# Two x loads ahead of two weight loads, and the pooling's constants in large buffers: a one-layer encoder block on one Trainium2 core

## The chip, the core and the metric

The kernel runs on one core of a Trainium2 chip. A core has five engines that run side by side, each with its own in-order queue of instructions: TensorE (PE in the profile; its weight loads are listed apart as PEld), VectorE (DVE), ScalarE (ACT), GpSimd (POOL) and SyncE (SP). Here SP issues nearly all transfers from device memory, and sixteen DMA engines carry them out. Matmul results go into PSUM banks; everything else lies in the core's on-chip memory, called SBUF.

The metric is the device time of one execution in microseconds (us); lower is better. The time before is 1462.05 us, the median of three runs (1461.95 to 1462.69).

## The reference, cut to what matters

One layer, 256 positions of 2048 channels in float32. The input is normalised, multiplied by one wide matrix into seven parts, mixed by a pooling branch and a retention branch, gated, projected, added, and followed by a gated feed-forward part:

```python
u = rmsnorm(h, norm_mix)
z = u @ w_in                                  # 2048 x 11264
p, q, k, v, g_ret, g_pool_br, g_ret_br = jnp.split(z, split_idx, axis=-1)
y_pool = pool_branch(p, w_pool_group, pool_scale) @ w_pool_proj
y_ret = retention_branch(q, k, v, g_ret, ret_gn_gain) @ w_ret_proj
merged = sigmoid(g_pool_br) * y_pool + sigmoid(g_ret_br) * y_ret
h = h + merged @ w_out
h = h + conv_glu(rmsnorm(h, norm_ffn), w_up, conv_w, conv_b, w_down)
out = rmsnorm(h, norm_final)
```

`rmsnorm` divides each position by the root of its mean square. `pool_branch` takes trailing means over 2, 4, 8 and 16 positions for four groups of channels, subtracts the token itself, and multiplies each group by its own 256x256 matrix.

## The kernel before

**Arithmetic.** Each float32 product is made of three matmuls. `split` (L95) makes a rounded copy `hi` on ACT (L96) and the remainder `lo` on DVE (L97); `mm3` (L103) does hi x hi, lo x hi and hi x lo (L104, L105, L106). In some places a Strassen scheme (`Pair.strassen`, L317) does seven block products instead of eight.

**The z stage.** The columns of `w_in` are taken in eleven pairs of 512-column blocks. Each pair runs over eight groups of 256 rows of weights; one group is one load of 1 MB (128 partitions x 2048 floats). `run_pair` (L370) does a pair: per group and per half (one 512-column block) it multiplies the two 128-row blocks of positions, `tb` 0 and 1, 12 matmuls of 128x512 for each half of a group. In a pair's last two groups the order is turned round: both groups for half 0, then both for half 1, 24 matmuls each. So the two PSUM banks of half 0 are complete 24 matmuls before the pair ends. There are four such banks (`acc`), all in use by one pair, and the next pair's first matmul needs one that has been emptied.

**The first pair** gives the first columns of q and k. It starts with the kernel and its eight groups of weights are loaded, with the transposed x, at the top (L192 to L222; `raws`). Its banks are emptied by four copies on ACT (L498) in `qk_pair`; the rotation of q and k (`rotate`, L510) comes later, since it needs the reciprocal root of the mean square of x.

**That mean square** comes from a second load of x, in the layout with positions on partitions. `x_squares(tb)` (L243) loads one half of x (1 MB, L245) into a large buffer and runs four squares with a sum on ACT (L248); for the second half it also issues the loads of three constant tables (`trig`, `ident`, `vecs`). `x_rms` (L254) adds up the sums, makes the reciprocal root on DVE in 16 small instructions, and scales the rotation's table with it (L260).

**When this is done in the program** is set by the queue `side`: `run_pair` calls `tick` (L139) after each group, and each tick runs the next entry of `side`. An empty entry lets one group pass:

```python
side.extend([lambda: None] * 4)
side.append(lambda: x_squares(0))
side.extend([lambda: None] * 2)
side.append(lambda: x_squares(1))
side.extend([lambda: None] * 2)
side.append(x_rms)
```

**From the program's order to the engines' order.** A scheduler takes the instructions by priority, which follows the program's order; weight loads and their splits are marked with a higher one (`weights_first`, L84; used by `halves_of`, L283), and so are results (`results_first`, L91). What comes out is a fixed order for each engine, and semaphores for what has to wait.

**Buffers.** Weights land in three buffers `raw` (pool `wraw`, L55), and are split into four `hi` and four `lo` buffers of half a group each (pool `wsplit`, L56). A load is issued when the buffer's last content has been split, and a split runs when PE has read the last content of its `hi` and `lo`. Everything large that lives longer lies in 18 buffers of 8 KB per partition (`unit()`, L68). Names in the trace are those of the program: `u` for a large buffer, `t` for a small one (512 floats), `acc` and `aux` for PSUM.

**The pooling** (L666 to L727) starts behind the pair that makes its input. It loads a small table (`cnt`), the pooling's matrix (768 KB, `pm_raw`) and the group weights (1 MB, `wg_raw`); both use `raw` buffers (L668, L672). The matrix is copied once on ACT (L671), the weights are split in two halves (L677). `pool(g)` (L681) and `mix(g)` (L706) then run from `side` in the next pair.

Of the kernel before, what the change touches and what calls it, by code (L numbers as in the profile page):

```python
# [8 lines left out]
F32 = mybir.dt.float32  # L9
# [7 lines left out]
P = 128  # L17
# [31 lines left out]
def tile_block(ctx: ExitStack, tc: tile.TileContext, ins, out):  # L49
# [5 lines left out]
    wraw = ctx.enter_context(tc.tile_pool(name="wraw", bufs=3))  # L55
# [8 lines left out]
    def nm(base):  # L64
        counter[0] += 1
        return f"{base}_{counter[0]}"

    def unit(dt=F32):  # L68
        return units.tile([P, UNIT], dt, tag="u", name=nm("u"))
# [67 lines left out]
    side = deque()  # L137
# [105 lines left out]
    def x_squares(tb):  # L243
        xs = unit()
        sp.dma_start(xs, ins["x"][tb])  # L245
        for c in range(4):
            junk = t2k()
            act.activation(junk, xs[:, c * NB : (c + 1) * NB], AF.Square, accum_out=ssq1[:, tb, c : c + 1])  # L248
        if tb:
            sp.dma_start(trig, ins["trig"])  # L250
            sp.dma_start(ident, ins["ident"])
            sp.dma_start(vecs, ins["vecs"])
# [385 lines left out]
        side.append(lambda: turn((2, 3)))  # L638


    side.extend([lambda: None] * 4)
    side.append(lambda: x_squares(0))
    side.extend([lambda: None] * 2)
    side.append(lambda: x_squares(1))
    side.extend([lambda: None] * 2)
    side.append(x_rms)
    for half in range(2):
        qk = [unit(F32R), unit(F32R)]
# [16 lines left out]
    flush()  # L665
    cnt = const.tile([P, 4, 16], F32, tag="cnt", name="cnt")  # L666
    sp.dma_start(cnt, ins["invcnt"])
    pm_raw = wraw.tile([P, 2048], F32, tag="raw", name="pm_raw")  # L668
    sp.dma_start(pm_raw[:, : 4 * 384], ins["poolmat"])
    pm = unit(F32R)  # L670
    act.activation(pm[:, : 4 * 384], pm_raw[:, : 4 * 384], AF.Copy)  # L671
    wg_raw = wraw.tile([P, 2048], F32, tag="raw", name="wg_raw")  # L672
    sp.dma_start(wg_raw, ins["w_pool_group"])
    wg_h, wg_l = unit(F32R), unit(F32R)
    for i in range(2):
# [491 lines left out]
```

## Time and profile before

| | |
|---|---|
| median of three runs | 1462.05 us |
| the profiled execution, its own time | 1462.85 us |
| span of the core in that execution | 1461.0 us |
| mean granted TensorE clock over the span | 0.996 |
| DMA: moved, mean rate | 291.22 MB, 199 GB/s |

The profile is of one execution. Its span is the time from the core's first to its last event, and the own time has 1.85 us around it. Times within the trace are counted from the span's start. The page gives each engine's busy time; a busy TensorE need not be at full speed, since matmuls overlap (a 128x512 matmul is listed at 0.39 us, while the next one starts 0.23 us behind it) and since the granted clock can fall. So waits and slow stretches are read in two ways: from the idle time that the trace puts ahead of an instruction, with the one that ended it, and from the distance between one matmul's start and the next. In the rows of SP the time is that at which a transfer is issued; when it landed is told apart.

### The profile page before, as it was taken

The numbers are of one execution on the slowest core, as the hardware profiler recorded it, in microseconds if no ns is written. First come the engines' busy times: TensorE is split into PE (matmuls) and PEld (weight loads), VectorE is DVE, ScalarE is ACT, GpSimd is POOL, SyncE is SP. The second block draws the span as 40 slices with busy tenths as digits, with TensorE's granted clock in tenths as the row PEclk, the third lists the DMA queues.
The fourth block names the chain that finished last, engine by engine and source line by source line (L and its number), as shares of the span: only waits on it lengthen the run. The fifth ranks groups of instructions, "written<-read, shape, count | busy, mean of one in ns | idle before, by whom it ended". The sixth has DMA issues, their size and how long they took to land.

```text
span 1461.0 us, 18727 instructions
## 1 busy us (share of the span) xinstructions
PE 1446.0 (99%) x7163; PEld 1222.9 (84%) x7163; DVE 1179.1 (81%) x1638; ACT 794.6 (54%) x1023; POOL 0.2 (0%) x4
## 2 busy tenths in 40 slices
PE   9899999999999999999999999999999999999997
PEld 7788888888888888888888888888888888888886
DVE  6768797987888888988877777777777778888877
ACT  6555654555655554545564554555455445555553
POOL 0000000000000000000000000000000000000000
PEclk9999999999999999999999999999999999999999
DMA  8664456455456556565565554554555456655663
GB/s 317 218 216 173 144 202 223 173 169 227 148 199 222 210 177 219 185 227 214 194 227 183 206 188 173 201 201 174 183 207 187 173 202 237 223 204 187 228 210 122
DMA packets 43289, 291.22 MB, mean 199 GB/s; under 512 B 4928, under 2 KB 5568, under 8 KB 9152
## 3 DMA queue, kind: packets, MB, share of 16 engines
q1 hardware_dynamic: 42480, 288.73, 55.1%
q10 hardware_dynamic: 720, 1.31, 0.3%
q8 instruction: 56, 0.92, 0.2%
q14 instruction: 33, 0.27, 0.1%
HBM read 285.82 MB, written 4.19 MB: 198 GB/s over the span
## 4 chain that ended last, share of the span: by engine, by line
PE 96%; DMA 1%; DVE 1%; ACT 1%; issue 0%; SPq 0%; DVEq 0%; ACTq 0%
PE acc L879 22%; PE acc L104 15%; PE acc L106 15%; PE acc L105 15%; PE acc L887 11%; PE aux L104 6%; PE aux L105 6%; PE aux L106 6%; DMA raw<-in_w_in 1%; DVE lo L97 1%; ACT hi L96 0%; PE aux L526 0%; PE aux L745 0%; PE aux L805 0%; PE aux L623 0%
## 5 line engine op out<-in xcount | busy, mean ns | idle before, releaser
L96 ACT ACTIVATE hi<-raw 128x1024 fp32r<-128x1024 f32 (+1 forms) x522 | 545.7, 1052 | 410.8 <-PE acc L105 184.0
L97 DVE TENSOR_TENSOR lo<-raw,hi 128x1024 fp32r<-128x1024 f32 (+1 forms) x522 | 617.4, 1212 | 159.6 <-ACT hi L96 101.2
L104 PE MATMUL acc<-hi,u 128*128 128x512 f32 x926 | 363.6, 393 | 4.6 <-ACT t L498 3.8
L106 PE MATMUL acc<-lo,u 128*128 128x512 f32 x926 | 361.9, 391 | 0.5 <-DVE lo L97 0.5
L105 PE MATMUL acc<-hi,u 128*128 128x512 f32 x926 | 361.6, 390 | 0.0
L879 PE MATMUL acc<-u,hi 128*128 128x512 f32 x1408 | 328.4, 390 | 0.0
L879 PEld LDWEIGHTS acc<-u,hi 128*128 128x128 f32 x1408 | 261.3, 188 | 52.2
L104 PEld LDWEIGHTS acc<-hi,u 128*128 128x128 f32 x926 | 174.6, 189 | 42.3 <-ACT t L498 4.3
L106 PEld LDWEIGHTS acc<-lo,u 128*128 128x128 f32 x926 | 174.5, 188 | 38.7 <-DVE lo L97 2.3
L105 PEld LDWEIGHTS acc<-hi,u 128*128 128x128 f32 x926 | 174.6, 189 | 35.2
L887 PEld LDWEIGHTS acc<-u,lo 128*128 128x128 f32 x1408 | 174.8, 192 | 3.4
L887 PE MATMUL acc<-u,lo 128*128 128x256 f32 x1408 | 176.0, 283 | 0.0
L104 PE MATMUL aux<-hi,u 128*128 128x512 f32 x270 | 105.2, 390 | 0.0
L105 PE MATMUL aux<-hi,u 128*128 128x512 f32 x270 | 105.1, 389 | 0.0
L106 PE MATMUL aux<-lo,u 128*128 128x512 f32 x270 | 105.1, 389 | 0.0
L901 ACT ACTIVATE t<-acc 128x256 f32<-128x256 f32 x88 | 33.8, 384 | 99.9 <-PE acc L887 99.9
L96 ACT ACTIVATE u<-u 128x1024 fp32r<-128x1024 f32 x43 | 45.5, 1057 | 26.7 <-DVE u L304 21.1
L106 PEld LDWEIGHTS aux<-lo,u 128*128 128x128 f32 x270 | 50.7, 188 | 10.6
L104 PEld LDWEIGHTS aux<-hi,u 128*128 128x128 f32 x270 | 50.7, 188 | 10.5 <-ACT hi L96 0.2
L105 PEld LDWEIGHTS aux<-hi,u 128*128 128x128 f32 x270 | 50.7, 188 | 10.3
L96 ACT ACTIVATE four<-raw 128x512 fp32r<-128x512 f32 x43 | 27.1, 631 | 55.3 <-PE acc L105 20.7
L97 DVE TENSOR_TENSOR u<-t,u 128x256 fp32r<-128x256 f32 (+2 forms) x52 | 27.0, 527 | 37.0 <-ACT u L96 37.0
(183 smaller groups left out, 1127.8 us busy)
## 6 DMA issues: line engine op xcount, KB each, us to landing
raw<-in_w_up SPq DMA_DIRECT2D x88, 1024.0 KB, 5.1
raw<-in_w_in SPq DMA_DIRECT2D x85, 1024.0 KB, 4.9
raw<-in_w_down SPq DMA_DIRECT2D x44, 1024.0 KB, 4.9
raw<-in_w_ret_proj SPq DMA_DIRECT2D x16, 1024.0 KB, 4.9
raw<-in_w_out SPq DMA_DIRECT2D x16, 1024.0 KB, 4.9
raw<-in_w_pool_proj SPq DMA_DIRECT2D x8, 1024.0 KB, 4.9
u<-in_x SPq DMA_DIRECT2D x4, 1024.0 KB, 7.1
raw<-in_w_in SPq DMA_DIRECT2D x4, 512.0 KB, 7.9
```

The costliest lines, as they stand in the source:

```text
L96: act.activation(hi, src, AF.Copy)
L97: dve.tensor_tensor(lo, src, plain(hi), ALU.subtract)
L104: pe.matmul(o, ah, bh, start=start, stop=False)
L105: pe.matmul(o, al, bh, start=False, stop=False)
L106: pe.matmul(o, ah, bl, start=False, stop=stop)
L879: pe.matmul(o[half], w2[half][hf][0][:, i * P : (i + 1) * P], hview(kt), start=kt == 0, stop=False)
L887: pe.matmul(o[half][:, :T], wl, hview(kt)[:, :T], start=False, stop=kt == KT - 1)
L901: act.activation(small_part[:, half * T : (half + 1) * T], o[half][:, T:], AF.Copy)
```

## The change

Two edits. The first moves the two calls of `x_squares` in `side`: they ran at the fifth and eighth tick of the first pair, and now run at the third and fourth. The number of empty entries is chosen so that `x_rms` stays at the eleventh. The second takes `pm_raw` and `wg_raw` from the large buffers instead of the `raw` buffers.

```diff
-    side.extend([lambda: None] * 4)
+    side.extend([lambda: None] * 2)
     side.append(lambda: x_squares(0))
-    side.extend([lambda: None] * 2)
     side.append(lambda: x_squares(1))
-    side.extend([lambda: None] * 2)
+    side.extend([lambda: None] * 6)
     side.append(x_rms)
...
-    pm_raw = wraw.tile([P, 2048], F32, tag="raw", name="pm_raw")
+    pm_raw = unit()
     sp.dma_start(pm_raw[:, : 4 * 384], ins["poolmat"])
...
-    wg_raw = wraw.tile([P, 2048], F32, tag="raw", name="wg_raw")
+    wg_raw = unit()
     sp.dma_start(wg_raw, ins["w_pool_group"])
```

The order of TensorE's instructions stays as it was; the orders of SP, ACT and DVE differ at two places each. Numbers in the names below are those of the tiles (before and after the change the x tiles have other numbers; the weights have the same).

SP in the first pair, before: raw_220 is the last group of the first pair, raw_479, raw_535 and raw_583 are the first three of the second.

```order
L165 DMA raw_220<-in_w_in 128x2048
L273 DMA raw_479<-in_w_in 128x2048
L273 DMA raw_535<-in_w_in 128x2048
L245 DMA u_368<-in_x 128x2048
L273 DMA raw_583<-in_w_in 128x2048
L245 DMA u_426<-in_x 128x2048
L250 DMA trig<-in_trig 128x256
L251 DMA ident<-in_ident 128x128
L252 DMA vecs<-in_vecs 128x216
```

The same place of SP now:

```order
L165 DMA raw_220<-in_w_in 128x2048
L245 DMA u_320<-in_x 128x2048
L273 DMA raw_479<-in_w_in 128x2048
L245 DMA u_354<-in_x 128x2048
L250 DMA trig<-in_trig 128x256
L251 DMA ident<-in_ident 128x128
L252 DMA vecs<-in_vecs 128x216
L273 DMA raw_535<-in_w_in 128x2048
L273 DMA raw_583<-in_w_in 128x2048
```

Both halves of x and the three tables have moved ahead of raw_535, and the first half of x ahead of raw_479 as well.

ACT at the end of the first pair, before. t_439, t_441, t_467 and t_469 are the copies of the first pair's four banks: acc_244 and acc_246 hold half 0, acc_245 and acc_247 half 1. The rows with ssq are the squares.

```order
L96 ACTIVATE hi_537<-raw_535 128x1024
L248 ACTIVATE t_376,ssq_238<-u_368 128x512
L96 ACTIVATE hi_541<-raw_535 128x1024
L248 ACTIVATE t_428,ssq_238<-u_426 128x512
L248 ACTIVATE t_430,ssq_238<-u_426 128x512
L248 ACTIVATE t_432,ssq_238<-u_426 128x512
L248 ACTIVATE t_434,ssq_238<-u_426 128x512
L498 ACTIVATE t_439<-acc_244 128x512
L498 ACTIVATE t_441<-acc_246 128x512
L498 ACTIVATE t_467<-acc_245 128x512
L498 ACTIVATE t_469<-acc_247 128x512
```

The same place of ACT now (the squares of the first half of x stand further ahead, two on each side of the split hi_231<-raw_220, and the split of raw_479 comes just before these rows):

```order
L248 ACTIVATE t_356,ssq_238<-u_354 128x512
L248 ACTIVATE t_358,ssq_238<-u_354 128x512
L248 ACTIVATE t_360,ssq_238<-u_354 128x512
L248 ACTIVATE t_362,ssq_238<-u_354 128x512
L498 ACTIVATE t_439<-acc_244 128x512
L498 ACTIVATE t_441<-acc_246 128x512
L498 ACTIVATE t_467<-acc_245 128x512
L96 ACTIVATE hi_537<-raw_535 128x1024
L96 ACTIVATE hi_541<-raw_535 128x1024
L498 ACTIVATE t_469<-acc_247 128x512
```

The two splits of raw_535 stood ahead of the second half's squares and of all four copies; now they stand behind three of the copies and ahead of the fourth. On DVE the reciprocal root of the mean square has moved ahead of the two lo halves of raw_535.

SP at the pooling, before: raw_2773 is the last group of the pair ahead of it, raw_2882, raw_2916, raw_2966 and raw_3033 are the first four of the pair behind it.

```order
L273 DMA raw_2773<-in_w_in 128x2048
L669 DMA pm_raw<-in_poolmat 128x1536
L673 DMA wg_raw<-in_w_pool_group 128x2048
L273 DMA raw_2882<-in_w_in 128x2048
L273 DMA raw_2916<-in_w_in 128x2048
L273 DMA raw_2966<-in_w_in 128x2048
L273 DMA raw_3033<-in_w_in 128x2048
```

The same place now (u_2863 and u_2867 are the pooling's matrix and weights):

```order
L273 DMA raw_2773<-in_w_in 128x2048
L273 DMA raw_2882<-in_w_in 128x2048
L273 DMA raw_2916<-in_w_in 128x2048
L273 DMA raw_2966<-in_w_in 128x2048
L668 DMA u_2863<-in_poolmat 128x1536
L273 DMA raw_3033<-in_w_in 128x2048
L672 DMA u_2867<-in_w_pool_group 128x2048
```

The next pair's first three groups have moved ahead of both loads of the pooling. On ACT the copy of the matrix now stands between the two splits of raw_2916, and the splits of the pooling's weights behind those of raw_2966; before, all three stood ahead of the splits of raw_2916.

## The prediction, made before the change was timed

> **What bounds the kernel now.** I read the page first, then the waits of TensorE, then the order of time around each of them.
>
> ```profile
> span 1461.0 us, 18727 instructions
> PE 1446.0 (99%) x7163; PEld 1222.9 (84%) x7163; DVE 1179.1 (81%) x1638; ACT 794.6 (54%) x1023; POOL 0.2 (0%) x4
> ```
>
> ```profile
> PE acc L104 <- ACT t L498: 3.8, 1, 3.8
> PE acc L104 <- ACT hi L96: 0.8, 2, 0.6
> PE acc L106 <- DVE lo L97: 0.5, 1, 0.5
> ```
>
> PE is the bound: it is busy for 99% of the span, and the built order of its instructions is the same before and after the change. So only two things can move the time: places where PE waits, and places where it runs slowly. The second block is the list of waits (who <- waited for: total, times, longest); it names the waits for ACT and DVE that matter, one of 3.8 us and two or three short ones. DVE (81%), ACT (54%) and the transfers cost nothing except where they make one of these.
>
> The long wait, in PE's order of time (start, duration, instruction, idle time before it):
>
> ```profile
> 49.80 0.39 PE L105 MATMUL acc<-hi,u 128*128 128x512 f32 x1
> 50.02 0.39 PE L106 MATMUL acc<-lo,u 128*128 128x512 f32 x1
> 54.26 0.79 PE L104 MATMUL acc<-hi,u 128*128 128x512 f32 x1 [3.85 <-ACT t L498]
> 54.85 0.63 PE L105 MATMUL acc<-hi,u 128*128 128x512 f32 x1
> ...
> 59.97 0.46 PE L105 MATMUL acc<-hi,u 128*128 128x512 f32 x1
> 60.27 0.40 PE L106 MATMUL acc<-lo,u 128*128 128x512 f32 x1
> ```
>
> A 128x512 matmul starts every 0.227 us when nothing is in the way (49.80 to 50.02). The first pair of column blocks ends at 50.02, the first matmul of the second pair starts at 54.26, and from there to 59.97 they start every 0.43 us. The stage's windows (time, then PE busy, PEld, DVE, ACT, POOL, granted clock, DMA share) say why:
>
> ```profile
> 50.27:54.26 3.99, 0.14 (x1) 0.00 (x1) 1.65 (x4) 3.99 (x11) 0.00 (x0) 0.88 0.56 193
> 54.26:60.27 6.01, 6.01 (x14) 4.71 (x15) 5.49 (x22) 2.31 (x4) 0.00 (x0) 0.51 0.42 165
> ```
>
> In the wait ACT is busy all the time (3.99 of 3.99 us), and after it the granted clock is 0.51: the wait is paid a second time, in half-speed matmuls. What ACT did:
>
> ```profile
> 36.62 1.06 ACT L96 ACTIVATE hi<-raw 128x1024 fp32r<-128x1024 f32 x1 [1.66 <-PE acc L105]
> 39.34 1.06 ACT L96 ACTIVATE hi<-raw 128x1024 fp32r<-128x1024 f32 x1 [1.66 <-PE acc L105]
> 42.06 1.06 ACT L96 ACTIVATE hi<-raw 128x1024 fp32r<-128x1024 f32 x1 [1.66 <-PE acc L105]
> 44.78 1.06 ACT L96 ACTIVATE hi<-raw 128x1024 fp32r<-128x1024 f32 x1 [1.66 <-PE acc L105]
> 45.75 0.61 ACT L248 ACTIVATE t<-u 128x512 f32<-128x512 f32 x1
> ...
> 50.22 1.06 ACT L96 ACTIVATE hi<-raw 128x1024 fp32r<-128x1024 f32 x1 [0.98 <-PE acc L105]
> 51.19 0.61 ACT L248 ACTIVATE t<-u 128x512 f32<-128x512 f32 x1
> ...
> 53.64 2.02 ACT L498 ACTIVATE t<-acc 128x512 f32<-128x512 f32 x4
> ```
>
> L498 empties the pair's four PSUM banks, which the next pair needs. Two of them were full 24 matmuls before the pair's end (near 44.8), but the copies stand behind a weight split that waits for PE (50.22) and behind four squares of the second half of x. ACT's in-order queue makes this wait, not the data. Until 44.78 the same ACT idles 1.66 us before every split: there is room for squares earlier.
>
> The short waits are one place, near 342 us:
>
> ```profile
> 341.64 0.39 PE L106 MATMUL acc<-lo,u 128*128 128x512 f32 x1
> 342.67 0.50 PE L104 MATMUL acc<-hi,u 128*128 128x512 f32 x1 [0.63 <-ACT hi L96]
> 343.00 0.40 PE L105 MATMUL acc<-hi,u 128*128 128x512 f32 x1
> 343.93 0.50 PE L106 MATMUL acc<-lo,u 128*128 128x512 f32 x1 [0.53 <-DVE lo L97]
> 344.26 0.39 PE L104 MATMUL acc<-hi,u 128*128 128x512 f32 x1
> 344.49 0.40 PE L105 MATMUL acc<-hi,u 128*128 128x512 f32 x1
> ```
>
> Here PE waits for the halves hi_2918 and lo_2919 of the weight group raw_2916. ACT and SP show where they were (for SP the first number is the issue):
>
> ```profile
> 341.55 2.01 ACT L96 ACTIVATE hi<-raw 128x1024 fp32r<-128x1024 f32 x2 [1.26 <-DMA raw<-in_w_in]
> ```
>
> ```profile
> 315.98 0.33 SPq L669 DMA_DIRECT2D pm_raw<-in_poolmat  x1
> 320.64 0.33 SPq L673 DMA_DIRECT2D wg_raw<-in_w_pool_group  x1
> ...
> 327.04 0.33 SPq L273 DMA_DIRECT2D raw<-in_w_in  x1
> ...
> 336.65 0.33 SPq L273 DMA_DIRECT2D raw<-in_w_in  x1
> ```
>
> Of the three raw buffers two were held by the pooling's loads, so raw_2882 was issued at 327.04 and raw_2916 only at 336.65, when the halves of raw_2882 had been made; it landed as PE needed it.
>
> **The change, part by part.** Nothing is added or dropped: the same instructions, the same bytes, and PE's order is unchanged. What moves:
>
> (1) Two x loads, three constant tables and eight squares go forward. First their cover. By the built order x(0) is now issued right behind raw_220 and x(1) right behind raw_479:
>
> ```profile
> 25.49 0.33 SPq L165 DMA_DIRECT2D raw<-in_w_in  x1
> 30.81 5.77 SPq L273 DMA_DIRECT2D raw<-in_w_in  x2
> ```
>
> ```profile
> DMA to landing us min/median/max: 7.0/7.2/7.5
> ```
>
> So x(0) is issued near 25.9 and x(1) near 31.2. With the 7.5 us that an x load took at most (second block, of the line that loads x) they land by 33.4 and 38.7. ACT reaches x(0)'s squares at 37.6, behind the split of 36.62, and x(1)'s at 45.75: both are there. The weights that now follow an x load keep their cover too: raw_479 (30.81) lands by 38.3 even with an x load's 7.5 us, and its split stands at 42.06. raw_535 is issued at 36.3 (30.81 + 5.77 - 0.33), behind x(1) and 0.3 MB of tables; by 43.8 at the same price, wanted near 50.
>
> Squares start 0.61 us apart (four from 51.19 to 53.64). Two of x(0) go after the split of 36.62 and two after that of 39.34: 1.2 us each, into gaps of 1.66. The four of x(1) run from 45.75 to 48.2, then L498 empties the first bank by 48.8 and the second by 49.3. PE wants the first at 50.25 (50.02 + 0.23). **The wait is gone with some 1.5 us to spare**, and with it the stretch at half clock.
>
> What is late next? The third bank is full 6 matmuls before the end, at 48.9, and emptied by 49.9. Before the fourth now stand the two splits of raw_535; the second must wait for PE's 50.22, so the fourth bank is free by 50.2 + 1.0 + 1.0 + 0.6 = 52.3 (wanted 18 matmuls into the new pair, at 54.3). DVE now makes the reciprocal root before the two lo halves of raw_535:
>
> ```profile
> 53.76 0.16 DVE L256 TENSOR_REDUCE ss<-ssq 128x2 f32<-128x8 f32 x1 [1.23 <-ACT t L248]
> ...
> 56.94 0.48 DVE L260 TENSOR_SCALAR trig_r<-trig,y 128x128 f32<-128x128 f32 x2
> ```
>
> That chain takes 3.18 us, now from 48.3 to 51.5, and two halves at 1.15 us each follow (of the 1.2 that a row of lo shows, about 0.1 overlaps): 52.7 and 53.8, wanted at 56.2 and 58.9. Margins of 2 to 5 us; no new wait.
>
> Price: from 50.02 to 60.27 there are 15 starts to the next (14 in the second window's row and one). At 0.227 they take 3.40 us, and took 10.25: **6.85 us**.
>
> (2) The pooling's two loads leave the raw buffers. raw_2882 takes the place of 315.98, raw_2916 that of 320.64, sixteen us earlier than now. Then its first split waits only for a buffer that PE is reading: PE's last half pair before the stall is 24 matmuls, from 336.4 back to 331.0 it reads the old pair, and 12 matmuls in, near 333.7, the buffer is free. hi_2918 is then ready by 335 and lo_2919 by 337, against 341.87 when PE wants it. The pooling's matrix is now issued behind raw_2966, at 327.4; its copy on ACT (1.47 us) stands between the two splits of raw_2916, and the second of these is wanted 12 matmuls after the first, at 344.6. So the matrix may land as late as 342, 14.6 us after its issue; the longest landing above is 7.5. The pooling's weights and their copies come behind that and are wanted later still. The two loads now take two of the 18 large buffers; for one of them the built order waits for the last matmul of the retention, which PE does before the whole pair of blocks that ends here, so this costs nothing.
>
> Price: 341.64 to 344.49 are five starts, 1.13 us at 0.227, and took 2.85: **1.72 us**. Bounds: 0 if something else holds the halves up, 1.72 as PE shows no other loss there. I take all of it, as sixteen us of lead stand against a lateness of one.
>
> Sum: 6.85 + 1.72 = 8.57. The profiled execution took 1462.85 us (span 1461.0), 0.8 over the median of 1462.05. So 1454.3 for it, a span of 1452.4, and **1453.5** by the median.
>
> **Rivals.** *Only the first wait goes* (raw_2916's halves are late for another reason): 1462.05 - 6.85 = 1455.2. Against it: ACT's split waited for the transfer (1.26 us by its row), and the transfer for the buffer.
>
> *A rest of the first wait stays.* The squares of x(1) still stand right ahead of L498. If they slip by more than 1.5 us, PE waits for the excess w: 1453.5 + w. Whether the clock drops too is open: the profile has a wait of 0.63 us after which pitch and clock stay, and one of 3.85 after which they don't. The Trainium skill, "TensorE: Matmul & The Clock Gate", Part 1, has the clock halved after an idle window of about 3.4 us that runs freely; by it a w of up to 3 would cost only w, about 1456 at the most likely sizes, and no run here shows a wait between.
>
> *The change doesn't do what it says*: x comes earlier, but L498 stays as late as now, since it still follows all eight squares. Then only 1.72 goes: 1460.3, within 0.2%. Against it: the squares wait for x alone, and x is 7 us early.
>
> *Slower: a weight group that is late behind x.* Place: raw_535, behind which ACT now holds the copy of the fourth bank. If it lands at L, that bank is free at L + 2.6 (two splits and a copy), and PE, which wants it at 54.3, waits L - 51.7, plus 2.9 us of half clock once the wait is long (6.85 less about 4). It eats the whole gain of 8.6 from L = 57.4, which is 21 us after its issue. The page "DMA: Bandwidth & Descriptors" of the Trainium skill, "Queues, rings and completion order", says that an engine takes descriptors in ring order, so everything issued ahead does go first; here that is 1.3 MB. The rows above have no load over 7.5 us with 1 MB ahead, so I give it little.
>
> **How the numbers follow.** Both waits go: 82%, 1453.5 (1452.5 to 1454.5, by the spread of 0.7 us of the three runs). Only the first: 6%, 1455.2. A rest: 5%, up to 1457.5. Not what it says: 4%, 1460.3. Slower: 3%, 1465 or more. The range, 1451.5 to 1457.5, adds a us below for what the first case may gain beyond its two sums, and leaves out the last two cases. A measurement of this kernel can tell some 0.2% (2.9 us) from no change: faster 0.93, same 0.04, slower 0.03.
>
> **What would show it.** TensorE's list of waits should lose its row for L498 and the rows near 342 us; the granted clock should be 1.00 in the window from 50 to 60; L498's first copy should start near 48.2; the second pair's matmuls should start 0.227 us apart from 50.25 on. The squares of x(0) should lie in the gaps after 37.6 and 40.3. The prediction is wrong if PE has a new wait between 50 and 62 us (fourth bank, lo halves of raw_535) or between 325 and 355 in the old times (copy of the matrix), or if L498 still ends PE's wait.

## The result, and the profile after

| | before | after |
|---|---|---|
| median (runs, range) | 1462.37 us (4 runs, 1461.95 to 1463.80) | 1454.34 us (4 runs, 1454.30 to 1455.32) |
| the profiled execution, its own time | 1462.85 us | 1455.32 us |
| its span | 1461.0 us | 1453.5 us |

The ratio after to before is 0.9945 (95% interval 0.9928 to 0.9962): 8.0 us less. In a later set of runs, 5 of the changed kernel and 18 of the kernel before, all on one chip, it is 0.9949 (0.9937 to 0.9962): 1455.08 against 1462.23 us.

First the page of the changed kernel, its head:

```profile
span 1453.5 us, 18725 instructions
PE 1442.0 (99%) x7163; PEld 1221.0 (84%) x7163; DVE 1178.4 (81%) x1638; ACT 794.3 (55%) x1023; POOL 0.2 (0%) x4
```

Then TensorE's waits (who <- waited for: total, times, longest):

```profile
PE acc L104 <- ACT hi L96: 1.5, 2, 0.9
PE aux L181 <- DVE warm L176: 1.2, 1, 1.2
PE aux L834 <- DVE dg L833: 0.2, 1, 0.2
```

The row of 3.8 us for L498 is gone, and so is the one for `lo` (L97). The two waits left in the first row lie in the first 13 us of the program. The window from 50 to 60 us, where the wait and the slow stretch were (columns as in the prediction):

```profile
50.00:60.00 10.00, 10.00 (x46) 8.28 (x45) 9.62 (x23) 5.87 (x7) 0.00 (x0) 1.00 0.52 188
```

TensorE is busy all the time, at a granted clock of 1.00. Its order of time at the end of the first pair (last matmul at 50.68, first of the second pair at 50.90):

```profile
50.45 0.39 PE L105 MATMUL acc<-hi,u 128*128 128x512 f32 x1
50.68 0.39 PE L106 MATMUL acc<-lo,u 128*128 128x512 f32 x1
50.90 0.39 PE L104 MATMUL acc<-hi,u 128*128 128x512 f32 x1
```

And what ACT did there:

```profile
38.24 0.61 ACT L248 ACTIVATE t<-u 128x512 f32<-128x512 f32 x1
...
39.99 1.06 ACT L96 ACTIVATE hi<-raw 128x1024 fp32r<-128x1024 f32 x1 [0.43 <-PE acc L105]
40.96 0.61 ACT L248 ACTIVATE t<-u 128x512 f32<-128x512 f32 x1
...
46.40 0.61 ACT L248 ACTIVATE t<-u 128x512 f32<-128x512 f32 x1
...
48.85 1.55 ACT L498 ACTIVATE t<-acc 128x512 f32<-128x512 f32 x3
50.30 2.00 ACT L96 ACTIVATE hi<-raw 128x1024 fp32r<-128x1024 f32 x2
52.19 0.59 ACT L498 ACTIVATE t<-acc 128x512 f32<-128x512 f32 x1
```

Squares of the first half of x fill what used to be gaps: the split of 39.99 now waits 0.43 us for TensorE where it waited 1.66. Three of the four copies start at 48.85, ahead of the splits that wait for TensorE.

In the profiled execution the first pair stands 0.7 us later from 12 us on than in the prediction's times. The cause lies ahead of the change. TensorE of the changed kernel at 11 us:

```profile
11.12 0.39 PE L106 MATMUL acc<-lo,u 128*128 128x512 f32 x1
12.43 0.50 PE L104 MATMUL acc<-hi,u 128*128 128x512 f32 x1 [0.93 <-ACT hi L96]
```

The same place in the kernel before:

```profile
11.21 0.39 PE L106 MATMUL acc<-lo,u 128*128 128x512 f32 x1
11.75 0.50 PE L104 MATMUL acc<-hi,u 128*128 128x512 f32 x1 [0.16 <-ACT hi L96]
```

This wait for a split of the first weights comes before either x load is issued, and it differs from execution to execution: the later executions below have from nothing to 1.0 us at this place or at the first real matmul near 5.5 us. In all of them the last matmul of the first pair started between 49.32 and 50.68 us.

### The profile page after: what moved, and what is told of

The parts are those of the page before. It is cut to its first block, busy times and chain, and to the rows that moved or that the text cites. A ratio compares the mean times of both kernels' runs of the same rounds, so it can differ in the third digit from the quotient of the medians.

```text
span 1453.5 us, 18725 instructions
## 1 busy us (share of the span) xinstructions
PE 1442.0 (99%) x7163; PEld 1221.0 (84%) x7163; DVE 1178.4 (81%) x1638; ACT 794.3 (55%) x1023; POOL 0.2 (0%) x4
## 4 chain that ended last, share of the span: by engine, by line
PE 97%; DVE 1%; DMA 1%; ACT 0%; SPq 0%; issue 0%; DVEq 0%; ACTq 0%
PE acc L878 22%; PE acc L106 15%; PE acc L104 15%; PE acc L105 15%; PE acc L886 12%; PE aux L104 6%; PE aux L106 6%; PE aux L105 6%; DMA raw<-in_w_in 1%; DVE lo L97 1%; PE aux L804 0%; PE aux L526 0%; PE aux L744 0%; PE aux L623 0%; DVE u L351 0%; PE aux L687 0%
## 5 line engine op out<-in xcount | busy, mean ns | idle before, releaser
L97 DVE TENSOR_TENSOR lo<-raw,hi 128x1024 fp32r<-128x1024 f32 (+1 forms) x522 | 618.1, 1214 | 155.8 <-ACT hi L96 98.4
L97 DVE TENSOR_TENSOR u<-u,u 128x1024 fp32r<-128x1024 f32 x45 | 54.9, 1221 | 3.1 <-ACT u L96 3.1
```

Of the source, the lines that this page charges most:

```text
L97: dve.tensor_tensor(lo, src, plain(hi), ALU.subtract)
```

## The experiments

My theory was that of the prediction: two independent waits, the first with a stretch at half clock behind it. Each ratio below is against the kernel before on the same chip.

| kernel | median us (range, runs) | before us (runs) | ratio (95%) |
|---|---|---|---|
| x alone | 1456.17 (1455.98 to 1456.57, 5) | 1462.20 (27) | 0.9955 (0.9943 to 0.9968) |
| pooling alone | 1460.02 (1459.37 to 1462.14, 11) | same | 0.9985 (0.9976 to 0.9994) |
| matrix alone | 1460.51 (1459.49 to 1462.51, 11) | same | 0.9987 (0.9979 to 0.9996) |
| weights alone | 1460.34 (1459.37 to 1462.64, 11) | same | 0.9985 (0.9977 to 0.9994) |
| late squares | 1456.71 (1455.48 to 1457.29, 5) | 1462.23 (18) | 0.9961 (0.9948 to 0.9974) |
| copies held, 4 | 1457.77 (1456.64 to 1458.81, 6) | same | 0.9969 (0.9958 to 0.9980) |
| copies held, 8 | 1461.00 (1459.96 to 1461.82, 10) | same | 0.9991 (0.9982 to 1.0000) |
| after, again | 1455.08 (1454.16 to 1455.91, 5) | same | 0.9949 (0.9937 to 0.9962) |
| fetch alone | 1457.08 (1455.62 to 1459.54, 4) | 1462.62 (9) | 0.9964 (0.9951 to 0.9978) |
| copies held, 3 | 1454.33 (1454.20 to 1455.39, 4) | same | 0.9945 (0.9932 to 0.9959) |
| late squares and pooling | 1454.62 (1454.54 to 1456.78, 5) | same | 0.9951 (0.9938 to 0.9965) |

### The two parts apart

x alone: the edit of `side` without that of the pooling.

> Only the first part of the change: x is fetched and squared early, the pooling's loads stay in the raw buffers. My theory (the two parts are independent, each worth what its stall cost TensorE): 6.85 us less than before, a ratio of 0.9953; TensorE's row of 3.8 us for L498 is gone, the granted clock is 1.00 in the window from 50 to 60 us, and the pair of short waits near 342 us is still there (some 7 us earlier, still 1.7 us together). Rival (the short waits near 342 were an after-effect of the x loads, so this part alone takes both): 8.0 to 8.6 us less. Rival (the gain of 8.0 us that was measured is mostly the pooling's part): 2 us less or nothing.

Measured: 6.0 us less, and the wait for L498 and the half clock are gone. The stall of the pooling is where it was, shifted by 6.9 us (TensorE of this kernel):

```profile
334.71 0.39 PE L106 MATMUL acc<-lo,u 128*128 128x512 f32 x1
335.73 0.50 PE L104 MATMUL acc<-hi,u 128*128 128x512 f32 x1 [0.63 <-ACT hi L96]
336.06 0.40 PE L105 MATMUL acc<-hi,u 128*128 128x512 f32 x1
336.99 0.50 PE L106 MATMUL acc<-lo,u 128*128 128x512 f32 x1 [0.53 <-DVE lo L97]
```

The same two waits as before, 0.63 and 0.53: neither rival holds. The gain is 0.8 us under my 6.85, which the next run explains.

Pooling alone: the edit of `pm_raw` and `wg_raw` without that of `side`.

> Only the second part: the pooling's matrix and weights go to large buffers, x stays where it was. My theory: 1.72 us less than before, a ratio of 0.9988; the wait of 3.8 us for L498 and the stretch at half clock behind it stay word for word, the two short waits near 342 us are gone, and raw_2916 is issued some 9 us or more earlier than 336.65. Rival (something else holds those halves up, and the loss at 342 goes to another wait close by): no change in time, a new wait between 325 and 355 us.

Measured: 2.2 us less (interval 0.9 to 3.5), in line with 1.72; the two short waits are gone. The wait for L498 stayed at 3.85 us, but "word for word" was wrong for what follows it. TensorE of this kernel:

```profile
53.58 0.50 PE L104 MATMUL acc<-hi,u 128*128 128x512 f32 x1 [3.85 <-ACT t L498]
53.91 0.42 PE L105 MATMUL acc<-hi,u 128*128 128x512 f32 x1
54.15 0.61 PE L106 MATMUL acc<-lo,u 128*128 128x512 f32 x1
54.56 0.63 PE L104 MATMUL acc<-hi,u 128*128 128x512 f32 x1
...
57.12 0.60 PE L104 MATMUL acc<-hi,u 128*128 128x512 f32 x1
57.55 0.40 PE L105 MATMUL acc<-hi,u 128*128 128x512 f32 x1
57.79 0.39 PE L106 MATMUL acc<-lo,u 128*128 128x512 f32 x1
```

The first two matmuls after the wait still run at full pace, the slow pace of 0.43 us lasts from 54.15 to 57.55, then it is over, 3.4 us after it began. In the kernel before it lasted to 60. The windows give the same (the clock is the third number from the end). The kernel before:

```profile
53.00:61.00 8.00, 6.74 (x18) 5.30 (x19) 6.65 (x25) 3.72 (x9) 0.00 (x0) 0.57 0.39 137
```

The pooling alone:

```profile
54.00:58.00 4.00, 4.00 (x12) 3.11 (x11) 3.55 (x17) 0.99 (x4) 0.00 (x0) 0.57 0.53 207
```

A mean clock of 0.57 over 8 us is 6.9 us at half speed (0.43 x 8 x 2); over 4 us it is 3.4. **The same wait of 3.85 us was followed by two slow pieces of 3.4 us in one execution and by one in another.** The kernels with the matrix alone and the weights alone also had one (0.57 over 4 us). One piece costs TensorE 1.7 us if it is busy in all of it.

### One buffer or both

```diff
-    pm_raw = wraw.tile([P, 2048], F32, tag="raw", name="pm_raw")
+    pm_raw = unit()
```

> Of the second part only the matrix's buffer: pm_raw in a large buffer, wg_raw still in a raw one; x as before. My theory (raw_2916 was late because it had to wait for the third raw buffer to come round; one raw buffer given back is enough): the next group to be issued at 327.04 is then raw_2916 and not raw_2882, it lands at 334 to 335, its first half is wanted at 341.87: all of the 1.72 us go, as in the kernel with both. Rival (each of the two loads holds one buffer, and each buffer is worth its share): 0.86 us less. Rival (both have to leave): nothing.

The other kernel has the same edit for `wg_raw` alone.

> Of the second part only the weights' buffer: wg_raw in a large buffer, pm_raw still in a raw one; x as before. My theory as for the kernel with the matrix alone: either buffer given back is enough, 1.72 us less, and no wait of TensorE near 342. Rival (by share): 0.86 us less. Rival (the matrix is the one that counts, since it is issued first and copied first): nothing here, and all with the matrix alone.

Measured: 1.7 and 1.9 us less; neither kernel's TensorE has a wait near 340 us left. SP of the kernel with the matrix alone (start of the issue; raw_2882 and raw_2916 are the pair in the second row, the second of them right ahead of the matrix):

```profile
314.40 0.33 SPq L673 DMA_DIRECT2D wg_raw<-in_w_pool_group  x1
319.24 6.72 SPq L273 DMA_DIRECT2D raw<-in_w_in  x2
326.02 0.43 SPq L669 DMA_DIRECT2D u<-in_poolmat  x1
```

raw_2916 is issued at 319.24 + 6.72 - 0.33 = 325.6, against 336.65 before (about 335.2 if the 1.4 us are taken off by which this execution is ahead there: 1.1 by a shorter stretch at half clock, told above, and 0.3 by its start). Ten us earlier are enough, so one buffer given back does it; the rivals by share and by order fall by the traces: matmul by matmul, TensorE gains 1.73 to 1.74 us on the kernel before across the place near 342, in both these kernels and in the one with both buffers. The times alone could not tell 0.86 from 1.72.

### Queue or data

In the change, x comes earlier and the copies of L498 stand further ahead on ACT. Two kernels take these apart. The first moves the squares the other way, behind the whole first pair:

```diff
-    side.extend([lambda: None] * 4)
+    side.extend([lambda: None] * 11)
     side.append(lambda: x_squares(0))
-    side.extend([lambda: None] * 2)
     side.append(lambda: x_squares(1))
-    side.extend([lambda: None] * 2)
     side.append(x_rms)
```

> The other way round, on the kernel before: x is not fetched earlier but later (its squares are moved behind the whole first pair, with eleven empty places ahead of them), so that L498's copies stand ahead of all eight squares on ACT. The pooling's loads stay as before. My theory (the wait was the copies' place in ACT's queue, not late data): TensorE's row of 3.8 us for L498 is gone, the clock is 1.00 from 50 to 60 us, and the time falls by the 6.0 us that the early fetch alone gave: ratio 0.996 (0.9945 to 0.9965). Rival (what counts is that x is there early): nothing is gained, or the wait comes back later in the pair, where the reciprocal root is late for the rotation and its transposes: ratio 0.999 or more.

Measured: 5.5 us less (interval 3.8 to 7.6); no wait for L498, clock 1.00 from 50 to 60 us. ACT of this kernel, the copies one by one between the splits and all squares behind them:

```profile
43.20 0.60 ACT L498 ACTIVATE t<-acc 128x512 f32<-128x512 f32 x1 [0.53 <-PE acc L106]
...
50.74 0.58 ACT L498 ACTIVATE t<-acc 128x512 f32<-128x512 f32 x1
51.21 0.62 ACT L248 ACTIVATE t<-u 128x512 f32<-128x512 f32 x1
```

So x need not be early at all: what made the wait was the place of the copies in ACT's queue. The second kernel keeps the squares' entries and moves only the two loads (`x_load` takes the large buffer and issues the load, the first two lines of `x_squares` until then):

```diff
-    side.extend([lambda: None] * 4)
+    side.extend([lambda: None] * 2)
+    side.append(lambda: x_load(0))
+    side.append(lambda: x_load(1))
     side.append(lambda: x_squares(0))
```

> On the kernel before, only the two loads of x are issued at the third and fourth group; the squares keep their entries at the old fifth and eighth. The pooling's loads stay as before. My theory (the squares wait for x alone, so the scheduler sets them into ACT's gaps as soon as x is on its way): the same gain as with the whole first part, 6.0 us, ratio 0.9955 to 0.9965, no wait for the copies of acc. Rival (the squares' entries decide): the wait of 3.8 us stays, ratio 0.999 to 1.

Measured: 5.5 us less (interval 3.2 to 7.2), no wait for the copies. The loads alone bring it, since the scheduler sets the squares into ACT's gaps once x is issued (in this trace between the splits, from 37.13 us on). One of the four runs took 1459.54 us, at a mean granted clock of 0.997 where the other three have 0.998 or 0.999; it was not profiled, and why is open.

### What a rest of the wait costs

Three kernels put the copies of L498 later again, by extra work on ACT ahead of the last square of x: `k` copies of a quarter of x onto itself, which leave x as it is. `k` stands for 4, 8 or 3. The squares also get a higher priority, so that the extra work stays with them:

```diff
-        for c in range(4):
-            junk = t2k()
-            act.activation(junk, xs[:, c * NB : (c + 1) * NB], AF.Square, accum_out=ssq1[:, tb, c : c + 1])
+        with tc.high_priority(offset=400):
+            for c in range(4):
+                junk = t2k()
+                for _ in range(k if tb and c == 3 else 0):
+                    act.activation(xs[:, 3 * NB :], xs[:, 3 * NB :], AF.Copy)
+                act.activation(junk, xs[:, c * NB : (c + 1) * NB], AF.Square, accum_out=ssq1[:, tb, c : c + 1])
```

> The changed kernel with the copies of L498 held back on ACT: ACT does four copies of a quarter of x onto itself ahead of the last square (extra work that leaves x as it is), so that the first L498 copy starts near 51.8 us instead of 48.2 and TensorE waits some 2.0 to 2.4 us at the same place. Theory A (the clock is judged by windows of 3.41 us that run on by themselves, and a window with 84% of waiting halves it, one with 30% doesn't): a wait of 2.2 us covers at most 65% of a window; if that is below the bar, the wait costs only itself: 2.0 to 2.4 us over the changed kernel, 1456.3 to 1456.8, clock 1.00 throughout, all runs within 1 us. Theory B (any wait of 2 us brings one window at half clock): 1.7 us more, 1458 to 1458.5, or runs spread over the two by where the window fell.

Measured: 1457.77 us, 2.7 over the changed kernel on the same chip. TensorE of the kernel with four (L501 is its L498):

```profile
49.66 0.39 PE L106 MATMUL acc<-lo,u 128*128 128x512 f32 x1
52.07 0.50 PE L104 MATMUL acc<-hi,u 128*128 128x512 f32 x1 [2.02 <-ACT t L501]
```

Its windows:

```profile
50.00:52.00 2.00, 0.05 (x1) 0.00 (x0) 1.19 (x2) 2.00 (x5) 0.00 (x0) 1.00 0.99 418
52.00:57.00 5.00, 4.93 (x15) 3.90 (x16) 4.39 (x21) 2.00 (x5) 0.00 (x0) 0.66 0.68 228
```

A wait of 2.02 us, and behind it 3.4 us at half speed (0.34 x 5 x 2). Theory A had the bar too high: 2.02 of 3.41 us is 59% of a window, and that was enough here. Theory B in its second form, runs spread over two prices, fits. In this execution the wait cost 2.2 us (52.07 - 49.66 - 0.23) and the slow piece 1.7, 3.9 in all. The runs lie over 2.2 us, from 2.5 us above the lowest of the changed kernel to 2.9 above its highest, as they would if some had the slow piece and some had not. Only one was profiled, but the lowest run has a mean clock of 0.999, where the profiled executions with a slow piece have 0.997 or 0.996; one piece takes 0.0012 off the mean, so by this reading that run had none.

> As the kernel with four copies, with eight: TensorE's wait for L498 grows by 2.4 us to some 4.4 to 4.8 us, longer than the 3.85 of the kernel before. Theory A (windows that run on by themselves): the granted clock is 0.5 for 3.41 or 6.83 us exactly, wherever the wait began; the time is the changed kernel's + 4.6 for the wait + 0.7 to 3.4 for the half clock, 1460 to 1462, and the runs spread over 2 us or more as those of the kernel before do. Theory B (a fixed half-speed stretch starts when the wait is long enough, so that the price is the same each time): 1461.8, all runs within 1 us.

Measured: 1461.00 us, over a range of 1.9. TensorE waits 4.66 us, the windows of this kernel:

```profile
50.00:53.00 3.00, 0.00 (x0) 0.00 (x0) 1.22 (x1) 2.90 (x5) 0.00 (x0) 1.00 0.81 281
53.00:58.00 5.00, 3.63 (x10) 2.92 (x11) 3.58 (x19) 2.75 (x7) 0.00 (x0) 0.66 0.53 202
```

Again 3.4 us at half speed, though the wait was longer than in the kernel before, which had twice that. So the slow stretch does not grow with the wait. Theory B (the same stretch each time, all runs within 1 us of 1461.8) fits neither these runs nor the 6.9 us of the kernel before; theory A gave 1460 to 1462, where the runs lie.

> The changed kernel with three copies of a quarter of x onto itself ahead of the last square, one less than in the kernel that waited 2.02 us; the last square and two copies of L498 then stand ahead of the split that waits for TensorE. This uses up nearly the whole margin that the prediction gave (1.5 us between the first emptied bank and the matmul that wants it). My theory (the margin is real, below it nothing is lost): the first bank is empty within 0.2 us of the time at which it is wanted, the wait is 0 to 0.2 us, no half clock, 1454.2 to 1456 like the changed kernel, ratio 0.9945 to 0.9955. Rival (the copies for the third and fourth bank, now behind both splits, come late): a wait of 0.5 us or more six or twelve matmuls into the second pair, and with it a window at half clock: 1456.5 or more.

Measured: 1454.33 us, as fast as the changed kernel. ACT starts the first copies at 49.45:

```profile
49.45 1.06 ACT L501 ACTIVATE t<-acc 128x512 f32<-128x512 f32 x2
50.41 1.06 ACT L96 ACTIVATE hi<-raw 128x1024 fp32r<-128x1024 f32 x1
51.35 1.08 ACT L501 ACTIVATE t<-acc 128x512 f32<-128x512 f32 x2
```

and TensorE, which ends the first pair with the matmul of 49.71, hardly notices:

```profile
49.71 0.39 PE L106 MATMUL acc<-lo,u 128*128 128x512 f32 x1
50.09 0.50 PE L104 MATMUL acc<-hi,u 128*128 128x512 f32 x1
50.42 0.40 PE L105 MATMUL acc<-hi,u 128*128 128x512 f32 x1
```

The next matmul starts 0.38 us later instead of 0.23. The copies' start, measured against the pair's end, moved from 1.83 us ahead (48.85 against 50.68) to 0.26 ahead: nearly 1.6 us of delay cost 0.15. The margin was real, and its end is where the prediction put it.

### The changed kernel again, and the other way to the same end

> The changed kernel once more, with more runs, beside the kernel before on the same chip. If what spreads the runs of the kernel before (1461.0 to 1465.1) is the stretch at half clock behind the L498 wait, which differs from run to run, the changed kernel's runs lie within 1.3 us (1454.2 to 1455.5), and the difference of the medians is 7.7 to 8.0 us: 6.0 with x alone and 1.7 to 2.2 with the pooling alone. Rival (the spread comes from elsewhere in the program): a spread of 3 us here too.

Measured: 7.15 us between the medians, a little under the expected 7.7, within the interval (5.6 to 9.2); the runs lie over 1.75 us, more than the 1.3 expected, where 18 runs of the kernel before on this chip lie over 2.75. So the half clock is not all of the spread; the start of the program has a share of up to 1.4 us (the first pair ends between 49.32 and 50.68), and the execution profiled here waits 0.46 us near 617 us for DVE (L759), which no other profiled one does.

The last kernel has the late squares together with both of the pooling's loads in large buffers.

> The late squares (x_squares behind the whole first pair) together with the pooling's loads in large buffers: the other way to take both waits away. My theory (the two waits are all there is to gain, by whichever way they go): the late squares' 5.5 and the pooling's 1.7 to 2.1, so 1454.6 to 1455.2, within 1 us of the changed kernel on any chip, ratio 0.9945 to 0.9955. Rival (the early x loads cost the changed kernel something at the start of the program, where transfers are tight): 1452 to 1453.5, ratio below 0.994, which would beat both.

Measured: 1454.62 us, 8.0 less than before and 0.3 above the kernel with three copies on the same chip, which runs like the changed one. Two different orders with both waits gone end at the same time. No kernel here beats the changed one by more than the runs differ.

## Why the prediction was right, by its steps

**What bounds the kernel.** TensorE's own order, with its waits and its clock, decided the time in every profiled execution: each of the two waits went with the edit that was meant for it and stayed with the other, and no other engine became the bound.

**The x loads and the squares.** x(0) and x(1) were foreseen at 25.9 and 31.2 us and were issued at 26.55 and 31.83, which is the same with 0.7 us of late start:

```profile
26.55 0.43 SPq L245 DMA_DIRECT2D u<-in_x  x1
31.46 0.33 SPq L273 DMA_DIRECT2D raw<-in_w_in  x1
31.83 0.43 SPq L245 DMA_DIRECT2D u<-in_x  x1
```

They took longer than the 7.5 us that I had as the most (the line's answer in the changed kernel):

```profile
DMA to landing us min/median/max: 8.1/8.2/8.3
```

With 8.3 they are there at 34.9 and 40.1, and ACT begins their squares at 38.24 and 46.40: still ahead by 3 us and more. The first copy was foreseen at 48.2 and came at 48.85 - 0.7. The fourth copy stands behind the two splits of raw_535, as foreseen, and ends at 52.8; it is wanted 18 matmuls after 50.90, at 55.0. Nothing new became late.

**The pooling.** The two rows near 342 are gone. SP of the changed kernel, with raw_2916 first and raw_2966 second in the upper row:

```profile
314.46 6.73 SPq L273 DMA_DIRECT2D raw<-in_w_in  x2
321.24 0.43 SPq L668 DMA_DIRECT2D u<-in_poolmat  x1
```

In the kernel before the same instants stand 6.85 - 0.7 = 6.15 us later: raw_2916 at 320.6 and the matrix at 327.4, the very times that the prediction gave. The edit takes two buffers where one would do.

**The sum.** For the profiled execution 1454.3 us were worked out, for the median 1453.5; the medians are 1454.34 and 1455.08, both in the range, the second above the 1454.5 that closed the first case. Between the two profiled executions both terms hold. Set beside the same matmul of the kernel before, one of the changed kernel is 0.65 us later at 38 us, 6.24 earlier at 63 us, 6.18 earlier at 333 us and 7.91 earlier at 356 us (times of the kernel before): 6.89 us for the first term and 1.73 for the second.

By the medians the parts alone gave 6.0 and 1.7 to 2.2 us where 6.85 and 1.72 stood. For the median the mis-sized term is the first: of its 6.85 us, 4.0 are the wait, and 2.84 are the stretch at half clock, which was read off one execution. It had two slow pieces; three other executions with the same wait had one, worth at most 1.7. With one piece the first term is 4.0 + 1.7 = 5.7, with two 6.85, and the 6.0 between the medians lie between. The step that failed with it is the last one, "0.8 over the median of 1462.05": that surplus was taken as lying outside the change, and 0.8 was taken off once more. If part of it was the second slow piece, the change had removed it already, and 1454.3 was the better number for the median too. That the unprofiled runs differ for this reason is inferred from their times and from four profiled executions with the wait, and the mean clock that is on record for every run supports it in part. Profiled, it was 0.996 with two slow pieces, 0.997 with one, 0.998 or 0.999 with none. Of the 54 runs of the kernel before in the experiments, 20 have 0.996 and average 1462.8 us, 26 have 0.997 and average 1461.8; eight have 0.998 and average 1462.5, which does not fit. The mean also takes in 3.3 to 6.4 us at half clock at the program's end, so it settles no single run.

**The rivals.** *Only the first wait goes* is excluded by the kernel with the pooling alone, *the change doesn't do what it says* by the window at clock 1.00. *Slower, a weight group late behind x*: raw_535 follows two loads that took 8.3 us, and its splits still ran in one piece at 50.30 with no wait for data. *A rest of the wait* had the mechanism right, but the lower of the two prices that it left open was wrong: a wait of 2.02 us was followed by 3.4 us at half speed and cost 3.9 in that execution, not only itself.

## What to carry to other kernels

Before an in-order engine is blamed on its load, look at what stands ahead of the instruction that is waited for: here the banks to be copied were full, and the copies stood behind a split that itself waited for TensorE and behind four squares. Moving the work in front earlier, or behind, gave the same within the spread of the runs.

A saving that is read from one execution belongs to that execution. Subtract it from that execution's own time, and carry its distance from the median along only if what is removed does not vary from run to run.

A short wait on TensorE isn't priced by its length alone: the two near 342 us, of 0.63 and 0.53, left the clock at 1.00, while one of 2.02 us brought a slow piece as long as that behind a wait of 4.66.

## What the runs showed of the clock

The half clock came in pieces of 3.4 us: one behind waits of 2.02, 3.85 and 4.66 us, two behind another of 3.85. Its start is not tied to the wait's end: in the pooling's kernel two matmuls ran at full pace first, in the kernel before it began within the wait. The windows' rows, cut to the pieces, show the clock at 0.50 in all of them; the kernel before:

```profile
53.28:60.11 6.83, 5.85 (x14) 4.59 (x15) 5.76 (x24) 3.13 (x7) 0.00 (x0) 0.50 0.46 161
```

The pooling alone:

```profile
54.15:57.56 3.41, 3.41 (x10) 2.63 (x9) 3.03 (x15) 0.82 (x2) 0.00 (x0) 0.50 0.57 223
```

The clock record in the traces shows windows that run on by themselves. In all thirteen profiled executions every change of the clock lies a whole number of windows of 3.413 us behind the first, the rise to full clock, which came 3.9 to 7.2 us after the span's start. In the six with a long wait the clock fell 47.79 us behind that rise each time, which is 14 windows, though the wait began anywhere from 43.4 to 45.2 us behind it. So what counts is how much of a window a wait fills (us; a wait begins where its idle time does):

| kernel | TensorE waits | half clock | waiting in the window that ends with the fall | waiting in the next window |
|---|---|---|---|---|
| before | 50.41 to 54.26 | 53.28 to 60.11 | 2.87 of 3.41 | 0.98 |
| pooling alone | 49.73 to 53.58 | 54.15 to 57.56 | 2.85 | 0 |
| matrix alone | 50.13 to 53.98 | 54.39 to 57.80 | 3.00 | 0 |
| weights alone | 49.98 to 53.83 | 53.38 to 56.79 | 3.40 | 0.45 |
| copies held, 4 | 50.05 to 52.07 | 52.63 to 56.04 | 2.02 | 0 |
| copies held, 8 | 49.71 to 54.37 | 53.92 to 57.33 | 3.41 | 0.45 |

A window with 2.02 us of waiting brought the fall; the window ahead of the fall in the pooling's kernel, with 1.00 (49.73 to 50.73), did not. At half clock a window with 0.45 us of waiting was followed by full clock, one with 0.98 by a second window at half clock. So the same wait of 3.85 us brought one piece or two by where it lay in the windows, and their place differs from execution to execution. These are single executions, one or two for each case.

The Trainium skill, "TensorE: Matmul & The Clock Gate", Part 1, describes just that, a window of 3413 ns that isn't started by the program; the lengths here agree. It also asks for about one idle window of 3.4 us before the clock falls. Here the measurement differs: 2.02 us were enough. Where the bar lies between that and the 1.00 us that left the clock alone was not tried.
